# The last quarter's attention probabilities: transposed on TensorE, or by DMA with VectorE and GpSimd, in a two-layer decoder trunk

## The chip, the cores and the metric

The kernel runs on one core of a Trainium2 chip. The metric is the device time of one execution in microseconds, median of several runs. The engines are called by their names in the profile: PE is TensorE's matmul (PEld its loading of weights into the array), DVE is VectorE, ACT is ScalarE, POOL is GpSimd, SP is the engine that issues nearly all DMAs.

## The reference

256 tokens, width 1024, two layers, all in fp32. The first layer's mixer is a dilated sliding-window attention, in three patterns (dilations 1, 4 and 16) whose softmaxes are merged by their log-denominators; the second layer's is a forgetting attention. Behind each mixer stands a SwiGLU network.

```python
def reference(x, ...):
    h = x
    for i in range(DEPTH):                       # 2
        if i % 2 == 0:
            h = h + dilated_mixer(rmsnorm(h, a_norm[j]), a_w_in[j], a_w_out[j])
        else:
            h = h + forgetting_mixer(rmsnorm(h, b_norm[j]), b_w_in[j], b_f[j], b_w_out[j])
        h = h + swiglu(rmsnorm(h, ffn_norm[i]), ffn_w_gu[i], ffn_w_down[i])
    return rmsnorm(h, final_norm)

def dilated_mixer(h, w_in, w_out):               # 16 heads of 64
    proj = (h @ w_in).reshape(B, S, 3, 3, 16, 64)
    ...                                          # scores, softmax, values of each pattern, merged
    return o.reshape(B, S, 1024) @ w_out
```

The change concerns the end of the dilated mixer: the transposing of the probabilities of the last four heads, and `o @ w_out`, the output projection.

## The kernel before

**Numbers.** Every fp32 operand of a product is kept as two fp32r tiles, a high part and the rest. `split` makes them: the high part is a copy by ScalarE (line 80), the low part a subtraction by VectorE (line 84). The names end in h and l: wh and wl for weights, oth and otl for the attention's output, xth and xtl for the normed input. A product (`mm3`) is three matmuls: high by high (line 203), then the two mixed ones (line 208).

**Weights.** `piece` loads a weight tile in two halves of 128x1024 (SP, line 101, tile raw, five buffers) and splits each; wh and wl have four buffers. Weights are asked for two tiles ahead of use. So SP, ScalarE and VectorE carry a steady run of loads, high parts and low parts between the other work, and each waits when its buffer is not yet free.

**Order.** The program order of each engine is fixed when the kernel is built, by a scheduler that takes the instructions in the order written, except for those under `first()`, which are put as early as what they read allows, and those under `issue_after`, which are put behind a given matmul. `later(i, fn)` puts a function in a list, `due`, that is called at step i.

**First attention.** The 16 heads go in four quarters of four heads, each as two pairs. For each quarter the projections of queries, keys and values are made, then the scores, and `softmax_a`: negated maximum (VectorE, line 497), exponential (ScalarE, line 289), reciprocal (line 500) and scaling (VectorE, line 508; ScalarE, line 506, for the first pair of the first three quarters). Each head's probabilities are one tile of 128x640: blocks 1 to 3 for dilation 1, blocks 0 and 4 for the dilated ones. The value tiles come out of PSUM by ScalarE (lines 263 and 281), and GpSimd moves the dilated values in sixteen copies of 32x256 (line 285).

The product with the values needs the probabilities transposed. In the first three quarters that goes by DMA, in `turn_a`: a DMA transposes 16-bit elements, so GpSimd first parts the low and high halves of each number (line 528), SP issues the transpose (line 530, 10 blocks of 128x128 for one head), and ScalarE puts the halves together again (line 531). In the last quarter TensorE transposes, in `trans_a`: ten transposes for a pair of heads (line 301), six into a PSUM bank called tr and four into one called o, and three copies out of PSUM (line 306, ScalarE twice, VectorE once). The transposed tiles have the name pt and lie in buffers of the tags pt (three) and bias (four).

`pv_a` multiplies probabilities by values: 24 matmuls for a pair (line 313) into one bank, which is then split into oth and otl, the k-tile number kt = 2 x quarter + pair. So the output projection's k-tiles 6 and 7 are the last quarter's.

**Output projection.** `out_proj` makes h = x + o @ w_out for two token halves, t0 and t1. Each half has two column halves n and eight k-tiles, so 16 products of 128x512 columns; t0 goes into two banks of the tag sc, t1 into two banks of the tag mm, which the projections of queries, keys and values used before. The second of these mm banks is the one from which the last value copies of line 263 read. With ks = 6 and done = 6 the order before is: six products of t0 (n = 0, k = 0 to 5), the transposes of pair 0, three products, the transposes of pair 1, three products, pv of both pairs, the four products of t0 with k = 6 and 7; then t1: four products, eight products, the transposes of the normed first half for the next stage (`norm_t`), four products. Each half ends with `residual` (line 654) and sums of squares (line 182).

Of the kernel before, what the change touches and what calls it, by code (L numbers as in the profile page):

```python
# [10 lines left out]
F32 = mybir.dt.float32  # L11
# [6 lines left out]
P = 128  # L18
# [14 lines left out]
def trunk(ctx: ExitStack, tc: tile.TileContext, T, out):  # L33
# [177 lines left out]
    def both(pair, *idx):  # L211
        return tuple(x[idx] for x in pair)
# [96 lines left out]
    def pv(o, v, kb, pr, w, n, start, stop):  # L309

        for h in range(2):
            c = kb * S + pr * P + h * HD
            nc.tensor.matmul(o[h * HD:(h + 1) * HD], v[:, c:c + HD], w(h), start=start, stop=stop)  # L313
# [193 lines left out]
                    else:  # L507
                        nc.vector.tensor_scalar(s, s, f, None, op0=ALU.mult)

    def trans_a(quad, pr):  # L510

        pt = quad["pt"]
        block = lambda h, i: pt[pr, h][:, i * P:(i + 1) * P]
        home = ("pt", "bias")[pr]
        quad["w", pr] = [transposed([block(h, 1 + qb) for h in range(2) for qb in range(2)], nc.scalar.copy, home=home),
                         transposed([block(h, 3) for h in range(2)], home=home),
                         transposed([block(h, b * 4) for h in range(2) for b in range(2)], nc.scalar.copy, "o", home)]

    def turn_a(quad, pr):

        quad["w", pr] = []
        bufs = {"pt": 3, "bias": 4}
        parts = lambda x: x[:, :640].bitcast(U16).rearrange("p (c t) -> p t c", t=2)
        for h in range(2):
            home = ("pt", "bias")[pr]
            w = ap.tile([P, 640 if home == "pt" else 6 * P], F32, tag=home, name="pt", bufs=bufs[home])
            split16 = w[:, :640].bitcast(U16)
            nc.gpsimd.tensor_copy(split16.rearrange("p (t c) -> p t c", t=2), parts(quad["pt"][pr, h]))
            turned = ap.tile([P, 6 * P], F32, tag="bias", name="turned", bufs=4)[:, :640].bitcast(U16)
            nc.sync.dma_start_transpose(turned.rearrange("p (g c) -> p g c", c=P), split16)  # L530
            nc.scalar.copy(parts(w), turned.rearrange("p (t c) -> p t c", t=2))
            quad["w", pr].append(w)

    def pv_a(quad, pr):
        vs, ws = quad["v"], quad["w", pr]
        o = psum("o")
        if len(ws) == 2:
            blocks = [w[:, :640].rearrange("p (i j) -> p i j", j=P) for w in ws]
            straight = lambda h: ws[h][:, P:3 * P]
            corner = lambda h: ws[h][:, 3 * P:4 * P]  # L540
            dilated = lambda h, a: blocks[h][:, 0:5:4, a * 32:a * 32 + 32]
        else:
            straight = lambda h: ws[0][:, h * S:(h + 1) * S]
            corner = lambda h: ws[1][:, h * P:(h + 1) * P]
            dilated = lambda h, a: halves(ws[2][:, h * S:(h + 1) * S], a)
        pv(o[:, :S], vs[0], 0, pr, straight, S, True, False)
        pv(o[:, P:S], vs[0], 1, pr, corner, P, False, False)
        halves = lambda x, a: x.rearrange("p (b n) -> p b n", b=2)[:, :, a * 32:a * 32 + 32]
        for a in range(4):
            pv(halves(o[:, :S], a), vs[1 + a % 2], a // 2, pr, lambda h: dilated(h, a), 64, False, a == 3)  # L550
        src = o[:, :S].rearrange("p (b a u) -> p b a u", b=2, a=4)
        kt = quad["hq"] * 2 + pr
        split(ot, lambda x: x[:, kt, :].rearrange("p (b u a) -> p b a u", a=4, b=2), src)
# [3 lines left out]
    def later(i, fn, *a):  # L557
        due.setdefault(i, []).append((fn, a))

    quads = [{"hq": hq, "fm": {}, "pt": {}, "v": {}} for hq in range(4)]  # L560
    for i, (hq, g, w) in enumerate(a_units):
# [19 lines left out]
        if w < 2:  # L581
            for c in range(2):
                if i == 3 and c == 0:
                    continue
                proj_feat(xt, wt, o[:, c * S:(c + 1) * S], c, (KT // 2, rstd_a) if i == 2 and c == 1 else None)
            if i == 2:
                values_12(quad["v"], lead)

                second = []
                wt = weights("a_in", 1, second)  # L590
                second.pop(0)()
                o_next = psum("mm")
# [12 lines left out]
            if i == 2:  # L605
                second.pop()(read)
            quad["fm"][g, w] = q
            if w == 1:

                j = i + (hq == 0)  # L610
                step = lambda hq: 9 * hq + 11 + 2 * (hq == 0)
                if g == 0:
                    later(step(hq - 1) + 2 if hq else j + 3, scores_0, quad)
                if g == 2:
                    later(j + 1, scores_12, quad)
                    later(j + 1, softmax_a, quad)
                    for pr in range(2):
                        if hq == 3:
                            later(step(hq) + pr, trans_a, quad, pr)
                        else:  # L620
                            later(j + 1, turn_a, quad, pr)
                    for pr in range(2):
                        later(step(hq) + 2, pv_a, quad, pr)
        elif g == 0 and hq > 1:
            for t in range(2):
                proj_tok(xt, wt, o[:, t * S:(t + 1) * S], t)
            quad["v"][0] = v_tile(o, r_a)
        elif i > 1:


            half = hq % 2 if g == 0 else g - 1
            if half == 0:

                lead = [psum("mm" if g else "o") for _ in range(2)]
            proj_pair(xt, wt, lead, half)
            if half and g == 0:
                vs = [v_tile() for _ in range(2)]
                for t in range(2):
                    v_pair(vs, lead[t], t, r_a[t])
                for y in range(2):  # L640
                    quads[hq - 1 + y]["v"][0] = vs[y]
            elif half:
                values_12(quad["v"], lead)
# [11 lines left out]
                parts.append(sq(hn[:, s]))  # L655
        return hn, parts

    def out_proj(nm, ot, h, grow, ks, done, banks):

        ws = [weights(nm, i) for i in range(4)]  # L660
        xt = xt_tile()
        res = []

        def part(t, acc, nk):
            last = None
            for n, k in nk:
                c = (k % 2) * D + n * 512
                last = mm3(acc[n], both(ot, ALL, k, slice(t * P, (t + 1) * P)),
                           both(ws[k // 2], ALL, slice(c, c + 512)), k == 0, k == KT - 1)
            return last  # L670

        def cols(ks):
            return [(n, k) for n in range(2) for k in ks]

        for t in range(2):
            acc = [psum(banks[t]) for _ in range(2)]
            if t == 0:

                nk = cols(range(ks))
                last = part(t, acc, nk[:done])  # L680
                nk = nk[done:]
                per = -(-len(nk) // (len(due) - 1))
                for i in sorted(due):
                    with tc.issue_after(last.ins):
                        for fn, a in due[i]:
                            fn(*a)
                    last = part(t, acc, nk[:per]) or last
                    nk = nk[per:]
                due.clear()
                part(t, acc, nk)  # L690
                last = part(t, acc, cols(range(ks, KT)))
            else:
                part(t, acc, cols(range(2)))
                with tc.issue_after(last.ins):
                    part(t, acc, cols(range(2, 6)))
                    norm_t(*res[0], grow, xt, 0)
                    part(t, acc, cols(range(6, KT)))
            res.append(residual(acc, h[t], f"h_{nm}{t}"))
        return res, xt


    def ffn(l, hs, xt, grow, mid):
# [106 lines left out]
        res.append(residual(acc[1], hs[1][0], f"hf{l}1") if l == 0 else (acc[1], hs[1][0]))  # L809
        return res  # L810

    g_f = load_grow(1)
    hs, xt = out_proj("a_out", ot, x, g_f, 6, 6, ("sc", "mm"))
    cst.tile([P, P], F32, name="gap")
    bf = cst.tile([P, NH], F32, name="bf")
    nc.sync.dma_start(bf, T["bf"].partition_broadcast(P))
# [189 lines left out]
        for fn, a in due.pop(i, ()):  # L1006
            fn(*a)
    g_f = load_grow(3)
    hs, xt = out_proj("b_out", ot, [h for h, _ in hs], g_f, 6, 9, ("mm", "sc"))

    def finish(t, h, parts):
        r = rstd(parts)
# [126 lines left out]
```

## Time and profile before

| | |
|---|---|
| median of 3 runs | 735.41 us (734.06 to 735.9) |
| profiled execution | 736.1 us |
| its span in the profile | 734.3 us |
| mean granted TensorE clock | 0.997 |
| TensorE's part of the chain that ended last | 97% |

The span runs from the first to the last instruction in the trace; 1.8 us of the profiled execution lie outside. In the rows a group is written as line, engine, operation, output<-inputs by the program's names, shapes and count; in the rows of a timeline the start and the duration in microseconds stand ahead, and in brackets the idle time before it with what ended it. Rows of waits give the waiting engine and tile, what released it, and the time in total, the count and the longest.

### The profile page before, as it was taken

Reading aid. Unit: us, or ns where it says so; the run is one execution under the profiler, and the core shown is the slowest. Engines: PE = TensorE matmul, PEld = TensorE weight load, DVE = VectorE, ACT = ScalarE, POOL = GpSimd, SP = SyncE. Lnnn points to the kernel's source line nnn. Section 1 sums busy time; section 2 is a strip of 40 time slices with the busy share of each in tenths; the row PEclk is TensorE's granted clock in tenths of the full one; section 3 lists DMA queues with packets and bytes.
Section 4 is the critical chain, followed back from the end, with each engine's and each line's share of the span. In section 5 each row is a group of like instructions: output and inputs, shape, how many; then the busy total and the mean of one; then the engine's idle time right before and its main releaser. Section 6 shows DMA issues by size and latency. Waiting matters only on the chain.

```text
span 734.3 us, 14310 instructions
## 1 busy us (share of the span) xinstructions
PE 726.4 (99%) x5856; PEld 672.4 (92%) x5856; DVE 495.9 (68%) x762; ACT 388.7 (53%) x617; POOL 83.0 (11%) x118
## 2 busy tenths in 40 slices
PE   9999999999999999999999999999999999999996
PEld 7999989999988899999999989999889999999995
DVE  6997998998996775554555474576776554556533
ACT  7646747738445663444554453587475444545421
POOL 0600206007105000000000004110010000000001
PEclk9999999999999999999999999999999999999998
DMA  9865955956864376656567352874547656656601
GB/s 335 306 202 174 237 182 153 289 193 152 268 194 160 116 241 221 195 179 203 195 202 247 127 168 90 294 260 138 172 142 237 222 179 203 195 188 218 198 1 58
DMA packets 55042, 141.93 MB, mean 193 GB/s; under 512 B 20257, under 2 KB 21441, under 8 KB 54977
## 3 DMA queue, kind: packets, MB, share of 16 engines
q1 hardware_dynamic: 54832, 140.88, 59.4%
q8 instruction: 46, 0.75, 0.4%
q14 instruction: 20, 0.16, 0.1%
q10 hardware_dynamic: 144, 0.15, 0.1%
HBM read 136.00 MB, written 1.07 MB: 187 GB/s over the span
## 4 chain that ended last, share of the span: by engine, by line
PE 97%; DVE 1%; ACT 1%; POOL 0%; issue 0%; POOLq 0%; DVEq 0%; ACTq 0%
PE ps_mm L208 34%; PE ps_mm L203 17%; PE ps_tr L208 9%; PE ps_sc L208 8%; PE ps_o L208 7%; PE ps_tr L203 5%; PE ps_sc L203 4%; PE ps_o L203 4%; PE ps_o L313 2%; PE ps_sc L395 2%; PE ps_tr L196 1%; PE ps_tr L301 1%; PE ps_sc L476 1%; PE ps_o L322 1%; PE ps_sc L894 0%; PE ps_sc L458 0%
## 5 line engine op out<-in xcount | busy, mean ns | idle before, releaser
L80 ACT ACTIVATE wh<-raw 128x1024 fp32r<-128x1024 f32 x236 | 243.4, 1054 | 207.1 <-PE ps_tr L208 66.7
L84 DVE TENSOR_TENSOR wl<-raw,wh 128x1024 fp32r<-128x1024 f32 x236 | 288.3, 1242 | 82.6 <-ACT wh L80 82.4
L203 PE MATMUL ps_mm<-xt,wh 128*128 128x256 f32 x816 | 227.2, 279 | 0.2 <-ACT v L281 0.2
L208 PE MATMUL ps_mm<-xt,wl 128*128 128x256 f32 x816 | 226.0, 277 | 0.0
L208 PE MATMUL ps_mm<-xt,wh 128*128 128x256 f32 x816 | 226.0, 277 | 0.0
L203 PEld LDWEIGHTS ps_mm<-xt,wh 128*128 128x128 f32 x816 | 153.1, 188 | 2.2 <-issue 1.7
L208 PEld LDWEIGHTS ps_mm<-xt,wl 128*128 128x128 f32 x816 | 153.6, 188 | 0.1
L208 PEld LDWEIGHTS ps_mm<-xt,wh 128*128 128x128 f32 x816 | 153.4, 188 | 0.0
L208 PE MATMUL ps_tr<-xt,wh 128*128 128x256 f32 x304 | 83.9, 276 | 0.0
L208 PE MATMUL ps_tr<-xt,wl 128*128 128x256 f32 x304 | 83.9, 276 | 0.0
L203 PE MATMUL ps_tr<-xt,wh 128*128 128x256 f32 x304 | 83.7, 276 | 0.0
L730 DVE TENSOR_TENSOR sa<-ps_tr,sa 128x256 f32<-128x256 f32 x38 | 16.1, 424 | 73.5 <-PE ps_tr L208 73.5
L208 PEld LDWEIGHTS ps_tr<-xt,wh 128*128 128x128 f32 x304 | 57.1, 188 | 0.0
L208 PEld LDWEIGHTS ps_tr<-xt,wl 128*128 128x128 f32 x304 | 57.0, 188 | 0.0
L203 PEld LDWEIGHTS ps_tr<-xt,wh 128*128 128x128 f32 x304 | 57.0, 188 | 0.0
L203 PE MATMUL ps_mm<-wh,xt 128*128 128x512 f32 (+1 forms) x144 | 49.8, 346 | 0.0
L173 POOL TENSOR_SCALAR rs<-ssq 128x1 f32<-128x1 f32 x7 | 1.9, 271 | 420.6 <-ACT junk L182 420.6
L208 PE MATMUL ps_mm<-wl,xt 128*128 128x512 f32 (+1 forms) x149 | 49.1, 335 | 0.0
L208 PE MATMUL ps_mm<-wh,xt 128*128 128x512 f32 (+1 forms) x149 | 49.1, 335 | 0.0
L285 POOL COPY v<-v 32x256 f32<-32x256 f32 x64 | 40.5, 632 | 71.2 <-ACT v L281 68.6
L203 PE MATMUL ps_sc<-wh,ah 128*128 128x512 f32 x80 | 31.4, 392 | 0.0
L208 PE MATMUL ps_sc<-wl,ah 128*128 128x512 f32 (+1 forms) x82 | 31.3, 385 | 0.0
(232 smaller groups left out, 1113.6 us busy)
## 6 DMA issues: line engine op xcount, KB each, us to landing
raw<-in_gu SPq DMA_DIRECT2D x88, 512.0 KB, 4.8
raw<-in_a_in SPq DMA_DIRECT2D x68, 512.0 KB, 5.0
raw<-in_dn SPq DMA_DIRECT2D x44, 512.0 KB, 4.7
raw<-in_b_in SPq DMA_DIRECT2D x24, 512.0 KB, 5.0
raw<-in_a_out SPq DMA_DIRECT2D x8, 512.0 KB, 5.0
raw<-in_b_out SPq DMA_DIRECT2D x8, 512.0 KB, 4.4
bias<-sums SPq DMA_DIRECT2D x8, 384.0 KB, 6.6
grow<-in_norms SPq DMA_DIRECT2D x4, 512.0 KB, 5.7
```

Of the source, the lines that this page charges most:

```text
L80: a = nc.scalar.activation(view(hi), src, AF.Copy)
L84: return nc.vector.tensor_tensor(view(lo), src, view(hi).bitcast(F32), op=ALU.subtract)
L196: nc.tensor.transpose(tr[:, k * P:(k + 1) * P], xn[:, kk * P:(kk + 1) * P], ident)
L203: nc.tensor.matmul(o, sh, mh, start=start, stop=False)
L208: last = nc.tensor.matmul(o[:, u], s, m[:, u], start=False, stop=end and u.stop == n)
L285: nc.gpsimd.tensor_copy(v[1 + a % 2][n:n + 32, a // 2 * S:a // 2 * S + S], by_t[a * 32:a * 32 + 32, t, g])
L301: nc.tensor.transpose(tr[:, i * P:(i + 1) * P], b, ident)
L313: nc.tensor.matmul(o[h * HD:(h + 1) * HD], v[:, c:c + HD], w(h), start=start, stop=stop)
L322: nc.tensor.matmul(o[:, :n], mhalf.to_broadcast([P, P]), mhalf.to_broadcast([P, n]), start=True, stop=True)
L395: nc.tensor.matmul(lead[t], xt[y][:, k, t * P:(t + 1) * P], w[z][:, u], start=k + y + z == 0, stop=k == KT - 1 and z == 1)
L476: nc.tensor.matmul(sc[h][c, o:o + 64], q[HR[h], pr, qb * P + a * 32:qb * P + a * 32 + 32], k[HR[h], pr].rearrange("p (b n) -> p b n", b=2) ...
L730: nc.vector.tensor_tensor(a, u, sg, op=ALU.mult)
```

## The change

`trans_a` is gone, and `turn_a` transposes in all four quarters. For the last quarter's second pair VectorE parts and joins the halves, for all other pairs GpSimd and ScalarE as before. The three steps now stand under `first()`. The tiles for the DMA's output come from both tags. `out_proj` takes a written list of the products ahead of the due functions. For the first attention that list has 16: t0 with k = 0 and 1, then 2 and 3 (eight products), t1 with k = 0 and 1 (four products), t0 with k = 4 and 5 (four products); then pv of both pairs, then the rest. For the second attention the list is what it was. In the changed kernel the parting copy is line 524, the DMA line 526, the joining copy line 527.

```diff
-    def trans_a(quad, pr):
-        ...
-        quad["w", pr] = [transposed([block(h, 1 + qb) for h in range(2) for qb in range(2)], nc.scalar.copy, home=home),
-                         transposed([block(h, 3) for h in range(2)], home=home),
-                         transposed([block(h, b * 4) for h in range(2) for b in range(2)], nc.scalar.copy, "o", home)]
     def turn_a(quad, pr):
+        own = quad["hq"] == 3 and pr == 1
+        apart_by, joined_by = (nc.vector.tensor_copy,) * 2 if own else (nc.gpsimd.tensor_copy, nc.scalar.copy)
+        home = lambda tag: ap.tile([P, 640 if tag == "pt" else 6 * P], F32, tag=tag, name="pt",
+                                   bufs={"pt": 3, "bias": 4}[tag])[:, :640]
         quad["w", pr] = []
         for h in range(2):
-            ...
-            nc.gpsimd.tensor_copy(split16.rearrange("p (t c) -> p t c", t=2), parts(quad["pt"][pr, h]))
-            turned = ap.tile([P, 6 * P], F32, tag="bias", name="turned", bufs=4)[:, :640].bitcast(U16)
-            nc.sync.dma_start_transpose(turned.rearrange("p (g c) -> p g c", c=P), split16)
-            nc.scalar.copy(parts(w), turned.rearrange("p (t c) -> p t c", t=2))
+            with first():
+                w = home(("pt", "bias")[pr])
+                apart = w.bitcast(U16)
+                apart_by(apart.rearrange("p (t c) -> p t c", t=2), parted(quad["pt"][pr, h]))
+                turned = home(("bias", "pt")[pr * (h == 0)]).bitcast(U16)
+                nc.sync.dma_start_transpose(turned.rearrange("p (g c) -> p g c", c=P), apart)
+                joined_by(parted(w), turned.rearrange("p (t c) -> p t c", t=2))
             quad["w", pr].append(w)
...
-                        if hq == 3:
-                            later(step(hq) + pr, trans_a, quad, pr)
-                        else:
-                            later(j + 1, turn_a, quad, pr)
+                        later(j + 1, turn_a, quad, pr)
...
+        for a, b in zip((0, *at), (*at, len(head))):
+            last = part(head[a:b]) or last
+            if due:
+                with tc.issue_after(last.ins):
+                    for fn, a in due.pop(min(due)):
+                        fn(*a)
...
+    def blocks(t, ks):
+        return [(t, n, k) for i in ks for n in range(2) for k in (2 * i, 2 * i + 1)]
...
-    hs, xt = out_proj("a_out", ot, x, g_f, 6, 6, ("sc", "mm"))
+    hs, xt = out_proj("a_out", ot, x, g_f, blocks(0, range(2)) + blocks(1, range(1)) + blocks(0, (2,)), (16,),
+                      ("sc", "mm"))
```

TensorE, in the output projection of the first attention, where the second block of transposes stood (ps_sc is a bank of t0, ps_mm one of t1):

```order
 L208 MATMUL ps_sc<-wh,otl 128x512
+L203 MATMUL ps_mm<-wh,oth 128x512
+L208 MATMUL ps_mm<-wl,oth 128x512
+L208 MATMUL ps_mm<-wh,otl 128x512
...
 L203 MATMUL ps_sc<-wh,oth 128x512
 L208 MATMUL ps_sc<-wl,oth 128x512
 L208 MATMUL ps_sc<-wh,otl 128x512
-L301 MATMUL ps_tr<-ident,p 128x128 x6
-L301 MATMUL ps_o<-ident,p 128x128 x4
```

Both blocks of ten transposes are gone, and the four products of t1 stand ahead of the last four of the list instead of behind pv.

ScalarE, from the last quarter's weight copies to the copies of pv's result (line 263 empties the bank of the last projection, v are values):

```order
 L80 ACTIVATE wh<-raw 128x1024 x2
+L527 COPY pt<-pt 128x2x640 x2
 L263 ACTIVATE v<-ps_mm,rs_a 128x256 x2
-L80 ACTIVATE wh<-raw 128x1024 x2
-L306 COPY pt<-ps_tr 128x512
-L306 COPY pt<-ps_o 128x512
-L306 COPY pt<-ps_tr 128x512
-L306 COPY pt<-ps_o 128x512
+L80 ACTIVATE wh<-raw 128x1024 x4
 L80 ACTIVATE oth<-ps_o 128x2x4x32 x2
```

The two joins of pair 0 stand ahead of the two value copies, and four weight halves instead of two stand between these and the oth copies.

VectorE, from the last scaling of the probabilities to the low parts of pv's result:

```order
 L508 TENSOR_SCALAR p<-p,c 128x384
-L84 TENSOR_TENSOR wl<-raw,wh 128x1024 x4
-L306 COPY pt<-ps_tr 128x256 x2
+L84 TENSOR_TENSOR wl<-raw,wh 128x1024
+L524 COPY pt<-p 128x1280 x2
+L84 TENSOR_TENSOR wl<-raw,wh 128x1024
+L527 COPY pt<-pt 128x2x640
+L84 TENSOR_TENSOR wl<-raw,wh 128x1024
+L527 COPY pt<-pt 128x2x640
+L84 TENSOR_TENSOR wl<-raw,wh 128x1024 x3
 L84 TENSOR_TENSOR otl<-ps_o,oth 128x2x4x32 x2
```

The four weight halves that stood in a row now stand between the copies, and two that stood behind the otl cuts stand ahead of them.

On SP the last quarter's four transposes stand between the weight loads of the next stage: two, then one weight load, then two. On GpSimd the two parting copies of pair 0 stand behind the ninth of the sixteen value copies (line 285). In the first three quarters the same copies, transposes and joins stand a few places earlier. Behind the output projection of the first attention the order is as before.

More of the change, by code (lines that the diff above doesn't have):

```diff
@@ L508, in softmax_a, with parted @@
                         nc.vector.tensor_scalar(s, s, f, None, op0=ALU.mult)
-    def trans_a(quad, pr):
-        pt = quad["pt"]
-        block = lambda h, i: pt[pr, h][:, i * P:(i + 1) * P]
-        home = ("pt", "bias")[pr]
-        quad["w", pr] = [transposed([block(h, 1 + qb) for h in range(2) for qb in range(2)], nc.scalar.copy, home=home),
-                         transposed([block(h, 3) for h in range(2)], home=home),
-                         transposed([block(h, b * 4) for h in range(2) for b in range(2)], nc.scalar.copy, "o", home)]
+    def parted(x):
+        return x.bitcast(U16).rearrange("p (c t) -> p t c", t=2)
     def turn_a(quad, pr):
+        own = quad["hq"] == 3 and pr == 1
+        apart_by, joined_by = (nc.vector.tensor_copy,) * 2 if own else (nc.gpsimd.tensor_copy, nc.scalar.copy)
+        home = lambda tag: ap.tile([P, 640 if tag == "pt" else 6 * P], F32, tag=tag, name="pt",
+                                   bufs={"pt": 3, "bias": 4}[tag])[:, :640]
         quad["w", pr] = []
-        bufs = {"pt": 3, "bias": 4}
-        parts = lambda x: x[:, :640].bitcast(U16).rearrange("p (c t) -> p t c", t=2)
         for h in range(2):
[L525 to L528, printed above, removed]
-            turned = ap.tile([P, 6 * P], F32, tag="bias", name="turned", bufs=4)[:, :640].bitcast(U16)
-            nc.sync.dma_start_transpose(turned.rearrange("p (g c) -> p g c", c=P), split16)
-            nc.scalar.copy(parts(w), turned.rearrange("p (t c) -> p t c", t=2))
+            with first():
[5 more added lines that the diff above has]
+                joined_by(parted(w), turned.rearrange("p (t c) -> p t c", t=2))
             quad["w", pr].append(w)
@@ L536, in pv_a @@
         o = psum("o")
[L537 to L541, printed above, removed]
-        else:
[L543 to L547, printed above, removed]
+        blocks = [w.rearrange("p (i j) -> p i j", j=P) for w in ws]
+        pv(o[:, :S], vs[0], 0, pr, lambda h: ws[h][:, P:3 * P], S, True, False)
+        pv(o[:, P:S], vs[0], 1, pr, lambda h: ws[h][:, 3 * P:4 * P], P, False, False)
         halves = lambda x, a: x.rearrange("p (b n) -> p b n", b=2)[:, :, a * 32:a * 32 + 32]
         for a in range(4):
-            pv(halves(o[:, :S], a), vs[1 + a % 2], a // 2, pr, lambda h: dilated(h, a), 64, False, a == 3)
+            pv(halves(o[:, :S], a), vs[1 + a % 2], a // 2, pr, lambda h: blocks[h][:, 0:5:4, a * 32:a * 32 + 32],
+               64, False, a == 3)
         src = o[:, :S].rearrange("p (b a u) -> p b a u", b=2, a=4)
@@ L617, in trunk @@
                     for pr in range(2):
-                        if hq == 3:
-                            later(step(hq) + pr, trans_a, quad, pr)
-                        else:
-                            later(j + 1, turn_a, quad, pr)
+                        later(j + 1, turn_a, quad, pr)
                     for pr in range(2):
@@ L656, in residual, with out_proj, part @@
         return hn, parts
-    def out_proj(nm, ot, h, grow, ks, done, banks):
+    def out_proj(nm, ot, h, grow, head, at, banks):
         ws = [weights(nm, i) for i in range(4)]
         xt = xt_tile()
-        res = []
-        def part(t, acc, nk):
+        accs = {}
+        done = set()
+        def part(items):
             last = None
-            for n, k in nk:
+            for t, n, k in items:
+                if (t, n, k) in done:
+                    continue
+                done.add((t, n, k))
+                if t not in accs:
+                    accs[t] = [psum(banks[t]) for _ in range(2)]
@@ L667, in part @@
                 c = (k % 2) * D + n * 512
-                last = mm3(acc[n], both(ot, ALL, k, slice(t * P, (t + 1) * P)),
+                last = mm3(accs[t][n], both(ot, ALL, k, slice(t * P, (t + 1) * P)),
                            both(ws[k // 2], ALL, slice(c, c + 512)), k == 0, k == KT - 1)
             return last
[L672 to L693, printed above, removed]
-                with tc.issue_after(last.ins):
[L695 to L698, printed above, removed]
@@ new lines, in out_proj @@
+        cols = lambda t, ks: [(t, n, k) for n in range(2) for k in ks]
+        last = None
+        for a, b in zip((0, *at), (*at, len(head))):
+            last = part(head[a:b]) or last
+            if due:
+                with tc.issue_after(last.ins):
+                    for fn, a in due.pop(min(due)):
+                        fn(*a)
+        last = part(cols(0, range(KT)))
+        res = [residual(accs[0], h[0], f"h_{nm}0")]
+        part(cols(1, range(2)))
+        with tc.issue_after(last.ins):
+            part(cols(1, range(2, 6)))
+            norm_t(*res[0], grow, xt, 0)
+            part(cols(1, range(KT)))
@@ L699, in out_proj @@
+        res.append(residual(accs[1], h[1], f"h_{nm}1"))
         return res, xt
@@ L1008, in trunk @@
     g_f = load_grow(3)
-    hs, xt = out_proj("b_out", ot, [h for h, _ in hs], g_f, 6, 9, ("mm", "sc"))
+    hs, xt = out_proj("b_out", ot, [h for h, _ in hs], g_f, [(0, n, k) for n in range(2) for k in range(6)], (9, 12),
+                      ("mm", "sc"))
     def finish(t, h, parts):
```

## The prediction

> **What bounds the kernel now.** I read the page's busy shares and its chain first, then TensorE's waits, then the stretch from 219 to 243 us, where the change works, engine by engine. All of the program after that stretch keeps its order. The page:
>
> ```profile
> PE 726.4 (99%) x5856; PEld 672.4 (92%) x5856; DVE 495.9 (68%) x762; ACT 388.7 (53%) x617; POOL 83.0 (11%) x118
> PE 97%; DVE 1%; ACT 1%; POOL 0%; issue 0%; POOLq 0%; DVEq 0%; ACTq 0%
> ```
>
> TensorE is the bound, and it hardly waits. So the time falls by what TensorE no longer does, and rises by each wait that it gets. VectorE (68%) and ScalarE (53%) have room on average; the change gives them work in one stretch of 15 us, and there the question is the order of each queue, not its load. TensorE in that stretch (start, time, matmul, count; each entry reaches about 0.17 us into the next, so pitches are taken between starts):
>
> ```profile
> 225.52 0.40 PE L203 MATMUL ps_sc<-wh,oth 128*128 128x512 f32 x1
> 225.75 0.40 PE L208 MATMUL ps_sc<-wl,oth 128*128 128x512 f32 x1
> ...
> 229.63 0.81 PE L301 MATMUL ps_tr<-ident,p 128*128 128x128 f32 x6
> 230.29 0.60 PE L301 MATMUL ps_o<-ident,p 128*128 128x128 f32 x4
> 230.64 0.48 PE L203 MATMUL ps_sc<-wh,oth 128*128 128x512 f32 x1
> 230.96 0.40 PE L208 MATMUL ps_sc<-wl,oth 128*128 128x512 f32 x1
> ...
> 232.81 0.82 PE L301 MATMUL ps_tr<-ident,p 128*128 128x128 f32 x6
> 233.47 0.60 PE L301 MATMUL ps_o<-ident,p 128*128 128x128 f32 x4
> ...
> 236.09 2.45 PE L313 MATMUL ps_o<-pt,v 128*64 128x256 f32 x48
> 238.47 0.50 PE L203 MATMUL ps_sc<-wh,oth 128*128 128x512 f32 x1
> ...
> 241.66 0.39 PE L203 MATMUL ps_mm<-wh,oth 128*128 128x512 f32 x1
> ```
>
> The first six products take 229.63 - 225.52 = 4.11 us, 0.685 each, 0.228 a matmul. A block of ten transposes: without it the second matmul of the next product would start at 229.63 + 0.23 = 229.86, and it starts at 230.96; the block costs 1.10 us. The four products after the 48 matmuls of "probabilities times values" (pv below) take 241.66 - 238.47 = 3.19 instead of 4 x 0.685 = 2.74: 0.45 us are lost there today on the two halves of the attention output.
>
> **What is removed.** Two blocks of transposes at 1.10 us, both in TensorE's chain: -2.2 us. Six copies out of PSUM go too, off the path.
>
> **What comes in, first link: pair 0.** GpSimd splits the 16-bit halves, SP transposes, ScalarE joins. Rows of the quarters that do so already, and of the neighbours:
>
> ```profile
> 168.48 2.66 POOL L528 COPY pt<-p 128x1280 uint16<-128x1280 uint16 x2 [38.70 <-DVE p L508]
> 224.40 0.43 POOL L285 COPY v<-v 32x256 f32<-32x256 f32 x1
> 169.84 5.19 SPq L530 DMA_TRANSPOSE turned<-pt  x3
> DMA to landing us min/median/max: 3.3/3.5/5.8
> 173.64 3.18 ACT L531 COPY pt<-turned 128x1280 uint16<-128x1280 uint16 x2 [0.33 <-DMA turned<-pt]
> 225.72 0.84 ACT L263 ACTIVATE v<-ps_mm,rs_a 128x256 f32<-128x256 f32 x2 [0.35 <-PE ps_mm L208]
> ```
>
> GpSimd's two copies now stand behind nine of the sixteen small value copies, so they start where the ninth ends, 224.83, and end at 226.2 and 227.5 (1.33 each). SP issues the transposes then; 3.5 us later, at 229.8 and 231.1, they have landed. ScalarE's joins take 1.53 each from start to start: 229.9 to 231.4, and 231.4 to 232.95.
>
> Behind these joins on ScalarE stand the two value copies of line 263, which run at 225.7 today. They empty the PSUM bank of the last projection, and the second bank of token half 1 is that bank. Its first product, the eleventh, now stands ahead of pv and waits for both. They end at 232.95 + 0.84 = 233.8. Without a wait the eleventh product would start at 225.52 + 10 x 0.685 = 232.37. So TensorE gets a new wait: +1.45 us. Its ends: with landings of 3.3 us it is 1.25; with the 5.8 us of the slowest row, or copies on GpSimd held up, 2.7 at most. I take 1.45, since no weight load stands between the copies and these transposes on SP. What is queued behind those joins on ScalarE besides (four weight halves, line 80) belongs to the next stage, which starts after token half 1, over 10 us later.
>
> **Second link: pair 1.** VectorE splits and joins. Its rows, and the queue around it:
>
> ```profile
> 223.74 1.74 DVE L508 TENSOR_SCALAR p<-p,c 128x256 f32<-128x256 f32 x4
> 225.41 5.41 DVE L84 TENSOR_TENSOR wl<-raw,wh 128x1024 fp32r<-128x1024 f32 x4
> 183.82 2.27 DVE L84 TENSOR_TENSOR wl<-raw,wh 128x1024 fp32r<-128x1024 f32 x1
> L916 DVE TENSOR_SCALAR p<-p,c_b 128x256 f32<-128x256 f32 x16 | 4.9, 348 | 0.1
> L1050 DVE TENSOR_SCALAR xn<-xn,rs 128x368 f32<-128x368 f32 x2 | 0.7, 406 | 0.5 <-POOL rs L1041 0.5
> L306 DVE COPY pt<-ps_tr 128x512 f32<-128x512 f32 x8 | 5.2, 686 | 6.1 <-PE ps_tr L301 6.0
> L306 DVE COPY pt<-ps_tr 128x256 f32<-128x256 f32 x2 | 0.8, 418 | 2.5 <-PE ps_tr L301 2.5
> ```
>
> No VectorE copy of this kind is in the trace. Operations with one operand, SBUF to SBUF: (406 - 348) / 112 = 0.52 ns an element, 348 - 256 x 0.52 = 215 ns fixed, so 1280 elements take 0.88 us. Copies out of PSUM: (686 - 418) / 256 = 1.05 ns, so 1.49 us. I take the first, because operand places match, and with GpSimd's value copies beside it 1.2 us for each split; 1.49 stays as the upper end. A weight subtraction takes 2.27 us against GpSimd's 16-bit copies, and 1.15 to 1.4 otherwise.
>
> VectorE then: the last scales, delayed by GpSimd's copies, to 226.4; one weight half to 228.7; the splits to 229.9 and 231.1; a weight half to 232.6. SP sends the pair's transposes at 229.95 and 231.6, but a weight load stands directly ahead of them, let go by the weight half that ends at 228.7. Where a transpose stood so before:
>
> ```profile
> 128.43 0.64 SPq L101 DMA_DIRECT2D raw<-in_a_in  x1
> 130.05 1.27 SPq L530 DMA_TRANSPOSE turned<-pt  x1
> ...
> 86.29 1.67 ACT L531 COPY pt<-turned 128x1280 uint16<-128x1280 uint16 x1 [0.20 <-DMA turned<-pt]
> 135.89 1.68 ACT L531 COPY pt<-turned 128x1280 uint16<-128x1280 uint16 x1 [1.75 <-DMA turned<-pt]
> ```
>
> That one landed 135.89 - 130.05 = 5.8 us after its issue. I take 5.5 for the first and 5.0 for the second: 235.5 and 236.6. The joins on VectorE: to 236.4; then a weight half in between; to 238.4. TensorE needs them for pv of pair 1. The sixteen products end at 225.52 + 16 x 0.685 + 1.45 = 237.95, pv of pair 0 takes half of the 2.4 us, so pair 1 starts at 239.15: the joins are 0.75 us ahead, and cost nothing; the cover is those 0.75.
>
> **Third link: the attention output.** After the second join three weight halves stand on VectorE ahead of the two otl cuts, which make the low half of pv's result. Two of them belong to the next stage and stood behind the cuts until now. A row without GpSimd beside it, and today's cut:
>
> ```profile
> 211.52 4.64 DVE L84 TENSOR_TENSOR wl<-raw,wh 128x1024 fp32r<-128x1024 f32 x4
> 238.15 0.62 DVE L84 TENSOR_TENSOR otl<-ps_o,oth 128x256 fp32r<-128x256 f32 x1 [4.05 <-ACT oth L80]
> PEld ps_sc L208 <- DVE otl L84: 0.4, 1, 0.4
> PEld ps_sc L203 <- ACT oth L80: 0.3, 1, 0.3
> ```
>
> At 4.64 / 4 = 1.16 each the three end at 241.9, so the first otl is ready at 242.5. The first product after pv would use it with its third matmul, at 240.35 + 2 x 0.228 = 240.8: a stall of 1.65 us where 0.45 is lost today: +1.2. Bounds: 0 if the pair lands in 3.5 us (the second join then ends near 236.6, the three halves at 240.1, otl at 240.7), +2.0 with copies of 1.49 us and the late landing. The value between is nearest to the rows of a transpose behind a load.
>
> **What else moves costs nothing:** in quarters 0 to 2 the same copies, transposes and joins change places by a few operations only, beside a TensorE that waits for none of them today; the row norm's transposes for the next stage come after 8 products instead of 12, 8 x 0.685 = 5.5 us, while the chain residual, squares, norm, which ends with this row, takes 244.40 + 1.42 - 241.66 = 4.2 from the start of token half 1:
>
> ```profile
> 244.40 1.42 DVE L191 SCALAR_TENSOR_TENSOR xn<-h_a_out,rs,grow 128x512 f32<-128x512 f32 x2 [0.69 <-POOL rs L176]
> ```
>
> If that slack were gone, TensorE would wait for the rest of it.
>
> **Sum:** -2.2 + 1.45 + 1.2 = +0.45 us. The profiled execution took 736.1 us (span 734.3 and 1.8 outside), 0.7 above the median of 735.4; so 736.55 for it, **735.9** against the median. A measurement of this kernel can tell about 0.3% (2.2 us) from no change.
>
> **Rivals.**
>
> *B, the loads don't delay the second pair* (28%). The third link falls away: -2.2 + 1.45 = -0.75, **734.7 us**. For it: the median landing is 3.5 us, and ten of twelve transposes with no load just ahead show it. Against: here a load is just ahead.
>
> *C, the full gain* (10%). The eleventh product finds its bank empty, and pv everything in place: -2.2, or up to -2.65 if the 0.45 lost today goes as well: **733.2 us** to 732.8. It needs the second join at 231.5, thus a landing at 230, 2.5 us after issue; the fastest row has 3.3. GpSimd could start earlier, if its nine value copies did; that is all that speaks for it.
>
> *D, pair 1 is late, and it is slower* (16%). One mechanism: VectorE's splits and joins take 1.49 us each instead of 0.88, so the second transpose goes out at 232.9, lands at 238.7 after 5.8 us, and its join ends at 240.2. pv of pair 1 waits 240.2 - 239.15 = 1.05. Three weight halves follow, to 243.7, otl to 244.3, needed at 240.8 + 1.05 = 241.85: 2.45 in place of 0.45, +2.0. Sum: -2.2 + 1.45 + 1.05 + 2.0 = +2.3, **737.7 us**. It gets slower than before from the point where the first otl is later than 240.8 + 0.45 + 0.75 = 242.0 us. For it: the VectorE copy is not in the trace. Against: operands in SBUF have run twice as fast.
>
> [...]
>
> A long wait could also cost clock. At the end of the program TensorE's last work ends by 727.6, and (stretch, length, busy us and counts of the engines, granted clock):
>
> ```profile
> 729.00:730.00 1.00, 0.00 (x0) 0.00 (x0) 0.59 (x2) 0.00 (x0) 0.80 (x2) 1.00 0.00 0
> 730.00:731.00 1.00, 0.00 (x0) 0.00 (x0) 0.73 (x2) 0.54 (x1) 0.01 (x1) 0.51 0.00 0
> ```
>
> The clock halves after some 2.4 us of idleness. [...]
>
> **How the numbers follow.** The forecast (A) has 46%, B 28%, C 10%, D 16%. The range leaves out most of C and what lies beyond D: from B with a landing of 3.3 us and the loss of 0.45 gone too (-0.95 - 0.45, and 0.4 of the measurement: 733.6) to D (737.7, and 0.1: 737.8). Faster by over 0.3%, below 733.2, only C can reach, most of it: 0.08. Slower by over 0.3%, above 737.6: D's upper part, three quarters of it with the clock: 0.12. The rest, 0.80, is within 0.3%.
>
> **What the new profile would show.** No line 301 for ten blocks at 229 to 234 us. If the first link is right, TensorE's waits have "ps_mm L203 <- ACT v" with 1.25 to 1.7 us, and the line 263 copies start near 233. If the second is right, VectorE's splits take 0.9 to 1.2 us and the second pair's transposes land over 5 us after their issue, without a TensorE wait for pt. If the third is right, "ps_sc L208 <- DVE otl" shows about 1.6 us. The forecast is wrong if the eleventh product doesn't wait, if pv waits for the joins, if otl is in time, or if any wait shows after 250 us that is not there today.

## The result and the profile after

| | before | changed |
|---|---|---|
| median, first measurement (6 runs each) | 735.45 us | 738.35 us |
| median, measured again in another group (29 and 11 runs) | 735.76 us | 738.15 us |
| profiled execution | 736.1 us | 738.19 us |
| its span | 734.3 us | 736.1 us |

The ratio is 1.004 (95% interval 1.0027 to 1.0053) in the first measurement and 1.0035 (1.0022 to 1.0047) in the second: the change made the kernel 2.4 to 2.9 us slower. The forecast was 735.9 us with a range from 733.6 to 737.8; both measurements lie above it.

TensorE does less, and the chain of work that ended last has less of it. The page of the changed kernel:

```profile
PE 724.8 (98%) x5836; PEld 669.8 (91%) x5836; DVE 502.3 (68%) x764; ACT 389.2 (53%) x615; POOL 88.2 (12%) x120
PE 81%; DVE 10%; DMA 3%; ACT 3%; issue 2%; SPq 0%; POOL 0%; POOLq 0%; DVEq 0%; ACTq 0%
```

Twenty instructions and 1.6 us are gone from TensorE, and it now waits for others. The waits of its weight loads in the changed kernel (in total, times, longest):

```profile
PEld ps_mm L203 <- ACT v L263: 1.9, 1, 1.9
PEld ps_sc L208 <- DVE otl L84: 1.5, 1, 1.5
```

Both were forecast, by name, with 1.25 to 1.7 and about 1.6 us. The timeline of the output projection in the changed kernel (TensorE, then ScalarE, VectorE and SP, with the landing of all sixteen transposes):

```profile
227.01 0.40 PE L203 MATMUL ps_sc<-wh,oth 128*128 128x512 f32 x1
...
235.53 0.50 PE L203 MATMUL ps_mm<-wh,oth 128*128 128x512 f32 x1 [1.53 <-ACT v L263]
...
239.83 2.45 PE L313 MATMUL ps_o<-pt,v 128*64 128x256 f32 x48
242.22 0.50 PE L203 MATMUL ps_sc<-wh,oth 128*128 128x512 f32 x1
...
243.99 0.50 PE L208 MATMUL ps_sc<-wh,otl 128*128 128x512 f32 x1 [1.04 <-DVE otl L84]
...
246.39 0.39 PE L203 MATMUL ps_mm<-wh,oth 128*128 128x512 f32 x1
...
255.45 0.39 PE L203 MATMUL ps_o<-wh,xt 128*128 128x512 f32 x1
```
```profile
233.16 1.62 ACT L527 COPY pt<-pt 128x1280 uint16<-128x1280 uint16 x1 [0.32 <-DMA pt<-pt]
234.65 0.82 ACT L263 ACTIVATE v<-ps_mm,rs_a 128x256 f32<-128x256 f32 x2
```
```profile
229.66 1.95 DVE L524 COPY pt<-p 128x1280 uint16<-128x1280 uint16 x2
237.22 0.91 DVE L527 COPY pt<-pt 128x1280 uint16<-128x1280 uint16 x1 [4.28 <-DMA pt<-pt]
239.15 0.90 DVE L527 COPY pt<-pt 128x1280 uint16<-128x1280 uint16 x1
239.93 3.48 DVE L84 TENSOR_TENSOR wl<-raw,wh 128x1024 fp32r<-128x1024 f32 x3
243.33 1.11 DVE L84 TENSOR_TENSOR otl<-ps_o,oth 128x256 fp32r<-128x256 f32 x2
```
```profile
231.08 0.64 SPq L101 DMA_DIRECT2D raw<-in_gu  x1
231.82 4.49 SPq L526 DMA_TRANSPOSE pt<-pt  x2
DMA to landing us min/median/max: 3.4/3.6/5.3
```

The eleventh product starts at 235.53 where 227.01 + 10 x 0.685 = 233.86 would be free: 1.67 us. The third matmul after pv starts at 243.99 where 242.22 + 0.46 would be free: 1.3 us. The four products after pv take 246.39 - 242.22 = 4.17 us, where the kernel before took 3.19: 0.98 us more. VectorE's copies take 0.9 to 1.0 us, and the second pair's first transpose, sent at 231.82 behind a weight load, lands 5.3 us later, the longest of the sixteen, and VectorE's join starts at 237.22. This stretch is much as forecast.

But it begins at 227.01 instead of 225.52. From the first product to the next stage's first product (255.45 - 227.01 = 28.4 us, before 253.44 - 225.52 = 27.9) the change costs 0.5 us, for which +0.45 was forecast. The larger part is lost ahead of it, in quarter 0. The next stage's first product, then VectorE, GpSimd and TensorE in quarter 0, before:

```profile
253.44 0.39 PE L203 MATMUL ps_o<-wh,xt 128*128 128x512 f32 x1
```
```profile
77.31 2.35 DVE L84 TENSOR_TENSOR wl<-raw,wh 128x1024 fp32r<-128x1024 f32 x2
80.23 0.66 DVE L443 TENSOR_TENSOR qk<-ps_mm,rcos 128x512 f32<-128x512 f32 x1
79.21 1.56 POOL L528 COPY pt<-p 128x1280 uint16<-128x1280 uint16 x1 [2.64 <-ACT pt L531]
97.73 2.45 PE L313 MATMUL ps_o<-pt,v 128*64 128x256 f32 x48
```

and in the changed kernel:

```profile
77.91 3.40 DVE L84 TENSOR_TENSOR wl<-raw,wh 128x1024 fp32r<-128x1024 f32 x2
81.88 0.68 DVE L443 TENSOR_TENSOR qk<-ps_mm,rcos 128x512 f32<-128x512 f32 x1
77.45 1.65 POOL L524 COPY pt<-p 128x1280 uint16<-128x1280 uint16 x1 [0.28 <-DVE p L508]
82.70 0.36 PE L203 MATMUL ps_mm<-xt,wh 128*128 128x256 f32 x1 [0.62 <-DVE qk L443]
99.83 2.39 PE L313 MATMUL ps_o<-pt,v 128*64 128x256 f32 x45
```

GpSimd's fourth parting copy used to wait 2.64 us, until ScalarE's first join had freed a buffer. In the change one transposed tile of the second pair lies in another buffer, so that wait is gone, and the copy runs at once: beside two weight subtractions on VectorE, which take 3.40 us together instead of 2.35. The rotation behind them (line 443) reads a PSUM bank, and TensorE waits for that bank: 0.9 us between two starts at 82.70 where 0.11 is the pitch, so 0.8 us. The product with the values (line 313) starts 2.1 us later than before. Some 0.6 us of this was lost in the first 26 us, where no instruction moved, and is not the change's; 0.8 us is the wait; the rest, about 0.6 us, is a slower pace of the matmuls behind it (last section). On the way to the output projection about 1.0 us comes back, because the kernel before ran a later stretch at the slower pace in its profiled execution, and 0.4 us more are lost. So the 1.5 us between the starts of the two output projections don't measure quarter 0; the experiments do.

### The profile page after: what moved, and what is told of

Its sections match the earlier page's. It is cut to its first block, busy times and chain, and to the rows that moved or that the text cites. A ratio compares the mean times of both kernels' runs of the same rounds, so it can differ in the third digit from the quotient of the medians.

```text
span 736.1 us, 14281 instructions
## 1 busy us (share of the span) xinstructions
PE 724.8 (98%) x5836; PEld 669.8 (91%) x5836; DVE 502.3 (68%) x764; ACT 389.2 (53%) x615; POOL 88.2 (12%) x120
## 4 chain that ended last, share of the span: by engine, by line
PE 81%; DVE 10%; DMA 3%; ACT 3%; issue 2%; SPq 0%; POOL 0%; POOLq 0%; DVEq 0%; ACTq 0%
PE ps_mm L208 27%; PE ps_mm L203 14%; PE ps_tr L208 9%; PE ps_o L208 7%; PE ps_sc L208 7%; PE ps_tr L203 5%; DVE wl L84 4%; PE ps_o L203 4%; PE ps_sc L203 4%; DMA raw<-in_a_in 1%; PE ps_o L313 1%; DVE p L508 1%; DVE p L293 1%; DMA otl<-in_lead 1%; DMA pt<-pt 1%
## 5 line engine op out<-in xcount | busy, mean ns | idle before, releaser
L80 ACT ACTIVATE wh<-raw 128x1024 fp32r<-128x1024 f32 x236 | 243.4, 1055 | 213.0 <-PE ps_tr L208 66.6
L84 DVE TENSOR_TENSOR wl<-raw,wh 128x1024 fp32r<-128x1024 f32 x236 | 291.6, 1256 | 81.3 <-ACT wh L80 81.2
```

What stands on the lines that cost most here:

```text
L80: a = nc.scalar.activation(view(hi), src, AF.Copy)
L84: return nc.vector.tensor_tensor(view(lo), src, view(hi).bitcast(F32), op=ALU.subtract)
```

## The experiments

Ratios are medians against runs of the kernel before on the same chip in the same group.

| kernel | median | before | ratio (95% interval) |
|---|---|---|---|
| changed, again | 738.15 | 735.76 | 1.0035 (1.0022 to 1.0047) |
| quarters 0 to 2 as before the change | 736.77 | 736.05 | 1.0012 (1.0004 to 1.0021) |
| before, with new quarters 0 to 2 alone | 736.87 | 736.05 | 1.002 (1.001 to 1.003) |
| changed, old buffers in quarters 0 to 2 | 736.97 | 735.76 | 1.0017 (1.0005 to 1.0029) |
| changed, half 1's products last | 738.16 | 736.05 | 1.0032 (1.002 to 1.0044) |
| changed, low weight halves behind otl | 737.18 | 736.05 | 1.0018 (1.0009 to 1.0028) |
| the same, and the load behind the transposes | 737.29 | 735.84 | 1.0017 (1.0005 to 1.0029) |
| changed, second pair by GpSimd and ScalarE | 739.98 | 735.84 | 1.006 (1.0041 to 1.008) |
| three edits together | 735.15 | 735.76 | 0.9993 (0.9979 to 1.0007) |
| four edits together | 733.55 | 735.76 | 0.9966 (0.9953 to 0.9979) |

The theory (T): the loss has two parts, quarter 0 (GpSimd's copy beside VectorE's subtractions) and the last quarter with the output projection (a chain through VectorE's queue). The rivals stand in each expectation.

**Quarters 0 to 2 undone.** The old function is used for them, the new one for the last quarter.

```diff
-                        later(j + 1, turn_a, quad, pr)
+                        later(j + 1, turn_a if hq == 3 else turn_old, quad, pr)
```

> The changed kernel, with the transposing of quarters 0 to 2 as it was before the change; only the last quarter has the new one. Theory T: 0.8 us of the loss comes from quarter 0, where GpSimd's fourth parting copy no longer waits for ScalarE's first join and so runs beside VectorE's weight subtractions; here that wait is back, so 0.8 us less than the changed kernel (738.35), about 737.5, and VectorE's two subtractions near 78 us take 2.35 together instead of 3.40. Rival R1, all of the loss is in the last quarter and the output projection: no difference, 738.3. Rival R2, the loss is spread and belongs to no part (placement of code, noise of the start): no difference either, 738.3.

736.77: +0.7 us above before (0.3 to 1.5) where the changed kernel has +2.4. More than half of the loss is in quarters 0 to 2, more than the 0.8 us of the one wait that T gave it. R1 and R2 fall.

**Quarters 0 to 2 alone.** The kernel before, with the new function for them.

> The kernel before, with the new transposing in quarters 0 to 2 alone; the last quarter transposes on TensorE and the output projection keeps its order. Theory T: 0.8 us slower than before (735.45), about 736.2, lost near 82 us. Rival R1: as before, 735.4. Rival R2: as before, within 0.2 us.

Slower by 0.8 us in the medians, ratio 1.001 to 1.003: 0.7 to 2.2 us. The two parts make +0.7 and +0.8 in their medians, by the ratios +0.9 and +1.5; the changed kernel has +2.4 to +2.9. They add up within their intervals. R1 and R2, for which nothing changes here, fall again. The wait is at the same place as in the changed kernel:

```profile
77.25 3.40 DVE L84 TENSOR_TENSOR wl<-raw,wh 128x1024 fp32r<-128x1024 f32 x2
76.79 1.65 POOL L533 COPY pt<-p 128x1280 uint16<-128x1280 uint16 x1 [0.27 <-DVE p L508]
82.05 0.35 PE L203 MATMUL ps_mm<-xt,wh 128*128 128x256 f32 x1 [0.63 <-DVE qk L443]
99.17 2.45 PE L313 MATMUL ps_o<-pt,v 128*64 128x256 f32 x48
```

**The changed kernel again**, as the reference of the next three.

> The changed kernel once more, beside the kernels of this group on one chip. Theory T: its two parts add up: quarters 0 to 2 cost 0.8 (by the trace) to 1.5 us (by the run with that part alone), the last quarter and the output projection 0.7 to 0.9 us; so 1.5 to 2.4 us slower than before. Rival R5, the first measurement of +2.9 us holds something that belongs to neither part: +2.9 us again.

+2.4 us: the upper end of the sum of the parts, within R5's interval too, so R5 isn't excluded by this run alone.

**Only the buffer.** The three steps stay under `first()`; the transposed tiles of quarters 0 to 2 go to the old buffers.

```diff
-                turned = home(("bias", "pt")[pr * (h == 0)]).bitcast(U16)
+                turned = home("bias" if quad["hq"] < 3 else ("bias", "pt")[pr * (h == 0)]).bitcast(U16)
```

> The changed kernel with one edit: in quarters 0 to 2 the transposed tiles all lie in the bias buffers again, while the three steps stay under first() as the change has them. Theory T: the fourth parting copy on GpSimd waits for ScalarE's first join again, VectorE's two subtractions near 78 us take 2.35 us again, and the loss of quarter 0 goes: 0.8 to 1.5 us less than the changed kernel. Rival R6, first() is the cause (ScalarE's fourth join stands a weight half earlier): no difference from the changed kernel, within 0.3 us.

1.2 us less than the changed kernel beside it. The intervals of the two ratios overlap, so the time alone doesn't exclude R6; the trace decides. GpSimd waits again, and VectorE is free of it:

```profile
77.04 2.35 DVE L84 TENSOR_TENSOR wl<-raw,wh 128x1024 fp32r<-128x1024 f32 x2
79.96 0.67 DVE L443 TENSOR_TENSOR qk<-ps_mm,rcos 128x512 f32<-128x512 f32 x1
78.93 1.57 POOL L524 COPY pt<-p 128x1280 uint16<-128x1280 uint16 x1 [2.62 <-ACT pt L527]
```

So it is the buffer, not `first()`. R6 falls. TensorE's wait at this place is in all seven profiles of kernels with the exchanged buffer (0.88 to 0.90 us between the two starts) and in none of the five with the old one (0.11). The wait that the buffer made was of use: it kept the copy away from the subtractions. In the changed kernel's trace the two subtractions take 3.40 us beside the copy of 1.65 us, 1.05 more than the 2.35 here. The copy ends there at 79.10; two subtractions that start when it ends would end at 79.10 + 2.35 = 81.45, by an estimate from these rows, and they end at 81.31. Why they take longer beside the copy, no run here shows.

**Half 1's products last.** The bank is asked for later.

```diff
...
-blocks(0, range(2)) + blocks(1, range(1)) + blocks(0, (2,))
+blocks(0, range(3)) + blocks(1, range(1))
...
```

> The changed kernel with one edit: the four products of token half 1 stand behind all twelve of token half 0, so the bank that ScalarE empties late is asked for 2.7 us later. Theory T: the wait of 1.7 us for that bank goes, but nothing is won, since VectorE's queue sets the end: pv of pair 1 then waits 0.8 us for the second join and the first product after pv waits for otl until the same moment, 243.9 on the clock of the changed kernel's trace: 738.3, within 0.3 us. Rival R3, the waits add up and each is paid by itself: 1.7 us less, 736.7.

738.16, ratio 1.0032 against 1.0035 to 1.004: nothing won, as T has it; R3 falls. The wait of 1.9 us for the bank went, and two others came or grew. TensorE's waits in this kernel:

```profile
PEld ps_sc L208 <- DVE otl L84: 1.9, 1, 1.9
PEld ps_o L313 <- DVE pt L527: 0.9, 1, 0.9
```

**Low weight halves behind the cuts.**

```diff
...
-        ws = [weights(nm, i) for i in range(4)]
+        lows = [] if nm == "a_out" else None
+        ws = [weights(nm, i, lows if i > 1 else None) for i in range(4)]
...
+        for low in lows or ():
+            low(quads[3]["cut"])
```

> The changed kernel with one edit: the two low weight halves of the next stage stand on VectorE behind the two otl cuts instead of ahead of them. Theory T: the otl cut comes 1.5 us earlier, TensorE's wait for it (1.3 us beyond the normal pitch) goes, and 737.0 is left. Rival R4, otl is late because its input oth is late (ScalarE, or pv itself): no more than 0.3 us less, 738.1.

The otl wait fell to what it was before the change, and the ratio to 1.0018, 1.2 to 1.6 us under the changed kernel's. R4 falls. VectorE in this kernel:

```profile
242.00 1.21 DVE L84 TENSOR_TENSOR wl<-raw,wh 128x1024 fp32r<-128x1024 f32 x1
244.10 0.63 DVE L84 TENSOR_TENSOR otl<-ps_o,oth 128x256 fp32r<-128x256 f32 x1 [0.90 <-ACT oth L80]
```

**The load behind the transposes as well.** SP's weight load between the two pairs is put behind them.

```diff
...
+            with behind_(sent[0] if key == ("gu0", 0) and c == 1 else None):
+                nc.sync.dma_start(raw, T[key[0]][key[1]][:, u])
...
```

> The changed kernel with two edits: the two low weight halves behind the otl cuts, and the weight load behind the second pair's transposes; the bank wait and quarter 0 are left as the change made them. Theory T: the second pair of transposes lands about 2 us earlier, but pair 1's joins were 0.9 us ahead of pv while TensorE loses 1.7 us at the bank, so the earlier landing is worth nothing here: within 0.4 us of the run with the low halves alone (1.1 us above before). Rival R9, the late landing costs time by itself: 1 us less than that run, so as before.

737.29, the same as without that edit: T. The joins came earlier (at 235.17 instead of 237.22 from nearly the same start), and TensorE still waited for the bank, 2.4 us here. R9 falls.

**Three edits, four edits.** The third is the old function in quarters 0 to 2, beside the two on products and low halves; the fourth is the load.

> The changed kernel with three edits: quarters 0 to 2 as before the change, token half 1's four products behind all twelve of token half 0, and the two low weight halves of the next stage behind the otl cuts. Theory T: the bank wait and the otl wait are both gone, and what is left is pv of pair 1 waiting 0.85 us for the second join, as the run with the products moved alone showed it: 2.2 won, 0.85 lost, up to 0.3 at the second otl: 1.0 us faster than before. Rival R3, nothing is left of the waits: 2.2 to 2.6 us faster. Rival R7, a wait that has not been seen takes their place: as before, or slower.

0.6 us under before in the median, the interval from -1.5 to +0.5. The one wait left in the stretch is the one forecast, 0.9 us of pv for pair 1's second join; the -1.0 of T is in the interval, R3's 2.2 is not; R7's "as before" isn't excluded by the time, but no unforeseen wait shows in this stretch of the trace.

> The kernel with the three edits and a fourth: SP issues the weight load that stood between the two pairs' transposes behind the second pair's. Theory T: the second pair then lands 3.5 us after its issue instead of 5.4, so its joins end 2 us earlier, pv of pair 1 waits for nothing, and 2.0 to 2.4 us less than before are left. Rival R8, the transposes of pair 1 are slow for another reason (those of pair 0 ahead of them): landing 5 us or more after the issue, and no more won than with three edits.

733.55: 2.2 us under before (1.5 to 3.5 by the ratio), so this version beats both kernels. The landing of the last quarter's four transposes with three edits, with four edits, then SP's transposes and VectorE's joins with four:

```profile
DMA to landing us min/median/max: 3.4/4.4/5.1
DMA to landing us min/median/max: 3.4/3.6/3.6
```
```profile
226.97 6.65 SPq L544 DMA_TRANSPOSE pt<-pt  x4
233.67 5.45 SPq L104 DMA_DIRECT2D raw<-in_gu  x4
```
```profile
229.26 1.95 DVE L542 COPY pt<-p 128x1280 uint16<-128x1280 uint16 x2
234.02 0.91 DVE L545 COPY pt<-pt 128x1280 uint16<-128x1280 uint16 x1 [1.48 <-DMA pt<-pt]
236.77 0.89 DVE L545 COPY pt<-pt 128x1280 uint16<-128x1280 uint16 x1
```

From the start of the splits to the first join it is 4.8 us here and 7.6 us in the changed kernel (237.22 - 229.66): the load directly ahead delayed the pair. None lands later than 3.6 us, R8 falls. No wait of pv for pair 1 is left.

**The second pair by GpSimd and ScalarE.** `own` is always false.

> The changed kernel with one edit: the last quarter's second pair goes by GpSimd and ScalarE as all others do, and VectorE copies nothing. Theory T: the queue that sets the end passes from VectorE to ScalarE: the second pair's joins end near 240.5 us there, three high weight halves follow, and oth, the high part of pv's result, is ready at 244 instead of 242, so TensorE waits for oth instead of otl, 0.3 to 0.8 us longer: 738.5 to 739.0 where the changed kernel has 738.2. Rival R10, VectorE's copies are what makes the third link late: without them the wait for otl goes and about 1.2 us are won, 737.0.

739.98, ratio 1.006: slower still, and R10 falls. The direction and the place are T's (oth is late now), the size is more than T's 0.3 to 0.8 us: TensorE waits for oth and for otl, the wait for the bank is 2.4 us instead of 1.9, and the profiled execution had half the clock for 6.8 us as well (last section).

```profile
PEld ps_sc L203 <- ACT oth L80: 1.7, 1, 1.7
PEld ps_sc L208 <- DVE otl L84: 1.3, 1, 1.3
```

## Why the prediction was wrong

**The step that failed** is "What else moves costs nothing: in quarters 0 to 2 the same copies, transposes and joins change places by a few operations only, beside a TensorE that waits for none of them today". They don't only change places: one buffer was exchanged, a wait on GpSimd went, and a copy met VectorE's subtractions, behind which TensorE then waits. The price stood in the prediction's own rows, 2.27 us for a subtraction beside a 16-bit copy of GpSimd, used there for the last quarter alone. The runs put what was taken as nothing at 1.2 us (only the buffer undone) and at 0.8 to 1.5 us (that part alone, by its medians and by its ratio). GpSimd's queue in quarter 0 has the same four copies in the same order in both profiles; the wait inside it stands in no order.

**Removed work**, -2.2 us: right. The four-edit version, where TensorE waits about 0.4 us each for oth and otl, much as before the change, has the stretch from first product to next stage at 252.19 - 226.25 = 25.9 us, 2.0 less than before.

**First link**, +1.45: mechanism and place right, measured 1.67 in the changed kernel. The 0.2 more fits ScalarE's second join, which waited 0.3 us for its transpose; it lies within the bounds 1.25 to 2.7. In the seven profiles that keep this wait it is 1.5 to 2.2 us, so 1.45 was low.

**Second link**, no wait for pair 1: right, as were the 0.9 to 1.0 us of VectorE's copies and the landing 5.3 us after issue (5.5 taken). The run with half 1's products last shows what the cover was worth: with the bank wait gone, pv waited 0.9 us.

**Third link**, +1.2: right in mechanism, 0.98 in size by the four products. The run with the low halves behind the cuts took it away.

**Sum of the stretch**: +0.45 forecast, +0.5 in the first profile. That it fits so closely is luck: the first link was 0.2 too small and the third 0.2 too large. In the four profiles that have the changed last quarter as it stands the stretch is 28.0 to 28.6 us, +0.0 to +0.7. What the total lacks is quarter 0, and what the executions' own spread adds.

**The rivals.** The result lies next to the time of D, but D's mechanism is not there: the copies took 0.9 us and pair 1 wasn't late. B's condition, no delay by the load, holds only where the load is moved; C's price, 733.2, was nearly reached by the four edits, not by the order that C has. The chance above 737.6 us counts on a loss of clock in D's upper part, and no run shows that loss: the clock stayed at 1.00 through the changed kernel's waits of 1.9 and 1.5 us, and fell in this stretch only in the profiled execution with the second pair on GpSimd and ScalarE, which cost some 2.9 us by an estimate (last section).

**What stays open.** With the last quarter transposed by DMA, some executions have more time outside the span: 1.7 to 3.4 us, where all of the kernel before and of quarters 0 to 2 alone have 1.7 to 1.9. In the first measurement the median is 2.25 us, some 0.45 of the +2.9, and no run here tells why. By their spans alone the medians are +2.2 us for the changed kernel again, -1.05 with three edits and -2.5 with four. TensorE also waits near 115 us for ScalarE's value copies (line 281): 0.35 us in the profile before, 0.47 and 0.34 in those of the changed kernel, 0 to 1.3 in the others, and 0.9 where quarters 0 to 2 are undone. It follows none of the edits, so a single profile can carry about a microsecond that isn't the change's.

## What to carry to other kernels

A buffer's wait can be a piece of schedule: when a change gives an operation another buffer, look for what it will now run beside, even in stages whose order doesn't change. When several waits end on one queue, taking away the first one moves the time to the next; sum them along the queue (here VectorE's: splits, joins, weight halves, cut), and move what nobody waits for behind what somebody does.

## What the runs showed of the hardware

**TensorE's matmuls went on at one of two paces, 0.113 or 0.118 us.** After the wait in quarter 0 the projection's matmuls came 4% slower until their shape changed, some 16 us later, with the granted clock at 1.00 and the same DMA share as before (0.81). Matmuls in two stretches of 12 us, before and after (length, busy time and count of PE first; behind the engines the granted clock, the DMA share and GB/s):

```profile
84.00:96.00 12.00, 12.00 (x108) 12.00 (x107) 12.00 (x20) 7.80 (x8) 0.00 (x0) 1.00 0.81 254
120.00:132.00 12.00, 12.00 (x104) 12.00 (x103) 12.00 (x16) 9.53 (x11) 8.06 (x8) 1.00 0.61 123
```
```profile
84.00:96.00 12.00, 12.00 (x105) 12.00 (x104) 12.00 (x20) 7.53 (x7) 0.00 (x0) 1.00 0.81 264
120.00:132.00 12.00, 12.00 (x108) 12.00 (x107) 10.61 (x14) 10.00 (x16) 10.42 (x13) 1.00 0.46 84
```

The kernel before ran its second stretch at the slower pace in that execution, behind a start 0.35 us late at 114.7, and the changed kernel its first. In starts of consecutive matmuls it is 0.113 and 0.118 us. In the profiles here with quarter 0's wait, four of seven went on at the slower pace; in the five without it none did. So a wait of 0.8 us could cost 0.6 us more (4% of 16 us). The second stretch, 27 us long, was slow in six of the twelve profiles, whatever the kernel, and moves an execution by 1.0 us. Why it picks one pace was not found.

**The clock fell when TensorE was idle for 1.8 us of 3.4.** In the profiled execution with the second pair on GpSimd and ScalarE, TensorE was idle for 1.56 and 0.91 us with 0.7 us of work between, and its clock fell inside the second wait:

```profile
240.88:244.29 3.41, 1.61 (x24) 1.01 (x20) 3.39 (x3) 2.86 (x4) 0.00 (x0) 1.00 0.30 99
244.29:247.70 3.41, 2.74 (x7) 2.18 (x8) 1.76 (x4) 0.00 (x0) 0.00 (x0) 0.50 0.75 263
247.70:251.11 3.41, 3.41 (x10) 2.67 (x9) 0.76 (x2) 1.39 (x4) 0.23 (x1) 0.50 0.29 111
251.11:254.52 3.41, 3.41 (x16) 2.81 (x15) 1.63 (x3) 0.06 (x1) 0.57 (x1) 1.00 0.00 1
```

At half the clock a matmul of 512 columns starts every 0.43 us instead of 0.23, which cost about 2.9 us until 251 us, by an estimate: 0.20 of every 0.43 us in the 6.15 us for which TensorE was busy at that clock. The half clock lasted 6.82 us here, twice 3.41; the full clock lasted 723.63 us in the kernel before and 727.04 in the changed one, 212.0 and 213.0 times 3.413. Cut into such steps, the traces show the clock fall after the step with 1.61 us of work above, and after one with 0.90 us at the end of the kernel before (726.61 to 730.02); it stayed at 1.00 after a step with 2.38 us in the changed kernel (241.80 to 245.22). The longest single wait with work on both sides, 2.02 us in the run with the load behind the transposes, was shared by two steps and left the clock at 1.00; the first of them:

```profile
232.06:235.47 3.41, 1.84 (x9) 1.18 (x7) 1.08 (x2) 3.00 (x4) 2.23 (x4) 1.00 1.09 206
```

No run was made to find how little work keeps the clock, and the ends of matmuls are modelled, so these are readings of single steps and not a rule. The prediction's 2.4 us of idleness was too long: 1.8 us within one step were enough here.
